# An fp32 encoder layer: operand splits moved between the steps of a projection, one product moved behind a transpose, and the last store halved

## The chip, the cores and the metric

The kernel runs on one core of one Trainium2 chip. The metric is the time of one execution on the device in microseconds (us). The kernel before took 962.0 us, the median of three runs (960.95 to 962.44). The engines are named as the profile names them: PE is TensorE, PEld its weight loads, DVE is VectorE, ACT is ScalarE, POOL is GpSimd, SP is SyncE, which issues nearly all the transfers.

## The reference

One encoder layer is applied to a prompt of 256 tokens and, with the same weights, to a sample of 2048 tokens. The model width D is 1024, every value is fp32. Cut to what matters:

```python
def fourier_mix(u, w_f, b_f):
    ug = u.reshape(b, s, 8, 64)
    spec = jnp.fft.fft2(ug, axes=(1, 3), norm='ortho')
    mixed = spec.real.reshape(b, s, 512)
    return mixed @ w_f + b_f

def encoder_layer(x, w_in, rpb, w_fourier, b_fourier, g_pre, g_na, g_f, w_out, g_post):
    h = rms_norm(x, g_pre)
    q, k, v, z_a, u_f, z_f = jnp.split(h @ w_in, 6, axis=-1)      # 512 columns each
    y_a = neighbourhood_attention(q, k, v, rpb)   # 8 heads of 64; grid 64 wide; window 8 rows x 16 columns
    y_f = fourier_mix(u_f, w_fourier, b_fourier)
    mixed = jnp.concatenate([rms_norm(y_a, g_na) * jax.nn.silu(z_a),
                             rms_norm(y_f, g_f) * jax.nn.silu(z_f)], axis=-1)
    return x + rms_norm(mixed @ w_out, g_post)
```

## The kernel before

**Products of two halves.** An fp32 operand is split into a high part, rounded to the type fp32r, and a low part, the rest. A product of two operands is then three matmuls (`mm3`, L163 to L166): high by high (L164), high by low (L165), low by high (L166). To split an operand, ACT casts it to the high part and DVE subtracts that from the source; the low part can be used when DVE is done. In the names of tiles an h or l at the end stands for the high or low part.

**The order of the work.** PE runs its work in the order in which the program is written. From L604 on this holds for ACT, DVE, POOL and SP as well: each takes its instructions strictly in the written order, and one that waits holds up all behind it on its engine. A helper such as `n_first` writes one instruction for ACT and one for DVE, so where it is called decides what stands behind it on two engines. Tiles come from pools of a fixed number of buffers, and a load into a reused buffer waits for the buffer's last reader.

**Stages by time.** Up to 94 us the first tiles are loaded and part of the values is computed. From 94 to 118.5 us come the prompt's products: a loop over b from 0 to 15, each round 24 matmuls of 256 columns. From 118.5 to 157 us `vu(0, ...)` makes v and u for a group of sample tokens, in 14 steps (j, s) of 12 matmuls of 512 columns. This is a fast scheme that needs seven products where eight would be usual, and j numbers them. Product j has an operand of tokens and an operand of weights:

- The operand of tokens j is written by `n_first(j)`: ACT casts `xh` at L434 and DVE subtracts `xl` at L435, both 128x2048. The source is one of the tiles `nx` and `nt`.
- The operand of weights j is loaded by `op_load(j)` (SP, L469, two halves) and split by `op_split(j)`: ACT L483 and DVE L484, two instructions of 128x1024 each, for j=5 L479 and L480 instead. The tiles are `vr` (raw), `vh` and `vl`.

Product j is first needed at step 2j. PE's results are added up by DVE at L511; finished tiles `vuo` are stored by SP at L354 (`vN`, `uN`). Besides, `rows_load` (SP, L295) brings further tokens `xm` and `rows_square` (ACT, L300) sums their squares. What is called between two steps stands in a table of hooks; within one step the hooks run behind the loads and splits of weights, in the order in which they were entered.

From 157 to 549 us the products for z, k and q and for the rest of the tokens follow. From 549 to 570 us comes the stage called Z here, the first part of the Fourier mix. `z_mm(g)` makes 16 matmuls into two PSUM tiles `ptb` (L1028), which are copied to `zt` (L1031), one by DVE and one by ACT (the first group: both by DVE). `z_turn(g)` transposes these (L1038, into `pab`) and splits the result (ACT L1004, DVE L1005). `z_32` (L1019) makes the one odd column and splits it (ACT L1009, DVE L1010). `pq(m)` multiplies the Fourier weights `wf` by a small matrix of cosines (m=0) or sines (m=1) with eight matmuls (L1081) into `ppq`. For m=1 each of its two halves is copied by ACT to `nq` (L1087), a row set of which POOL sends to `nw` by DMA (L1088); ACT then casts the scaled high part (L1089) and DVE makes the low part (L1090). The column of `nw` is cast at L1107 after `pq(0)`. At 570 us the products with these weights (`py`) start.

From 600 to 860 us the neighbourhood attention runs, from 860 us on the output products with the norm and the residual. `last_tile` ends the program: its second half is computed in two unequal parts to shorten the end, then `residual` (DVE L1758) makes x plus the scaled output for 512 columns and SP stores them (L1763), twice.

Of the kernel before, what the change touches and what calls it, by code (L numbers as in the profile page):

```python
# [168 lines left out]
def build(tc, A, O):  # L169
# [49 lines left out]
    def mmt(n):  # L219
        x = mmc[0] % 5 > 2  # L220
        mmc[0] += 1
        return ps.tile([128, n], F32, tag="t" if x else "a", name="mm", bufs=2 if x else 3)
# [10 lines left out]
    def gt(shape, dtype, name):  # L233
        return gp.tile(shape, dtype, tag="g", name=name)
# [12 lines left out]
    def k8(dtype, name, shape=(128, 4, 512)):  # L247
        return hp.tile(list(shape), dtype, tag="k8", name=name, bufs=NK)
# [142 lines left out]
    def n_load(x):  # L391
        if type(x) is tuple:
            nq[x] = k8(F32, "nx")
            nc.sync.dma_start(nq[x], A["xq"][0, x[0], x[1]])
            return
        nx = [k8(F32, "nx") for kh in range(2)]
        for kh in range(2):
            for b in range(2):
                nq[x, kh, b] = nx[kh][:, 2 * b:2 * b + 2]
                nc.sync.dma_start(nq[x, kh, b], A["xq"][1, kh, b][:, 2 * x:2 * x + 2])  # L400
# [30 lines left out]
    def n_first(j):  # L431
        src = nq[((0, 0), (1, 0), (0, 0), (0, 1), "t3", (1, 0), (1, 1))[j]]
        h, l = bnew[0, j] = [k8(F32R, "x" + x) for x in "hl"]
        nc.scalar.copy(h, src)  # L434
        nc.vector.tensor_tensor(out=l, in0=src, in1=f_(h), op=ALU.subtract)  # L435
# [22 lines left out]
    def r_put(x):  # L458
        nc.sync.dma_start(sD[x], (RU[1], RV[0], RU[0], RU[1], RV[1])[x])
# [3 lines left out]
    def op_load(j):  # L463
        if j < 2:
            l = [load(US, A["wv"][j][:, 2 * x:2 * x + 2], "vr") for x in range(2)]
        else:
            l = [gt(US, F32R, "vl") for x in range(2)]
            for x in range(2):
                nc.sync.dma_start(f_(l[x]), sD[(3, 2, 1, 0, 4)[j - 2]][:, 2 * x:2 * x + 2])  # L469
        op_[j] = [None, l]  # L470
# [228 lines left out]
    def wz_load(n):  # L699
        for x in range(n):  # L700
            wp_.append(load(BS, A["wz"][len(wp_)], "wr"))
# [59 lines left out]
    for b in range(16):  # L761
        kind, blk = divmod(b, 4)
        if 1 <= b < 10:
            wz_load(1)
        if b == 2:
            n_load((1, 1))
        if b in (5, 7):
            r_put(b // 2 + 1)
        if b == 10:
            op_load(0)  # L770
        if b == 12:
            op_load(1)
        if 2 <= b < 14:
            b_raw(b + 2)
        if 2 <= b < 8:
            x, y = divmod(b, 2)
            n_scale(None, *divmod(x, 2)[::-1], range(2 * y, 2 * y + 2))
        elif 8 <= b < 12:
            n_sum(b - 8)
        if b in (5, 12):  # L780
            n_first((5, 12).index(b) + 1)
        if b > 13:
            op_split(b - 14)
        p = mmt(512)[:, :TP]
        wh, wl = wb.pop(b)
        for k in range(KC):
            mm3(nc, p, wh[:, k], wl[:, k], hp_[:, k], lp_[:, k], k == 0, k == KC - 1)
        o = st.tile([128, 256], F32, tag="f", name="f", bufs=3)
        if kind % 2:
            i, d = p, o  # L790
        else:
            i = p.rearrange("p (b r c) -> p b r c", b=2, c=32)
            d = o.rearrange("p (r b c) -> p b r c", b=2, c=32)
        nc.scalar.activation(d, i, AF.Silu if kind < 2 else AF.Copy)
        if kind < 2:
            nc.sync.dma_start(zD[kind, blk * 128:blk * 128 + 128, :TP], o)
        else:
            nc.sync.dma_start((kD if kind == 2 else qD)[blk, :, :TP], o)

    def call(f, *a):  # L800
        return lambda: f(*a)
# [11 lines left out]
    def at(i, f, *a):  # L813
        hooks.setdefault(i, []).append(call(f, *a))

    for x, i in zip(range(3, 7), (0, 3, 5, 7)):
        at(i, n_first, x)
    for x in range(4):
        at(2 * x + 1, rows_load, x + 5)
        at(2 * x + 4, rows_square, x + 5)  # L820
# [19 lines left out]
    for i in range(16):  # L840
# [47 lines left out]
        for j in range(7):  # L888
            for f, d in ((u_load, 0), (u_split, 4), (u_stage1, 6)):
                x = 7 * pr + j - 7 - d  # L890
# [31 lines left out]
            if sg == 0:  # L922
                x, y = divmod(7 * (pr - 1) + j, 14)
# [99 lines left out]
    def z_mm(gq):  # L1023
        for x in range(2):
            for g in range(2 * x, 2 * x + 2):
                for m in range(2):
                    ms = slice(64 * m, 64 * m + 64)
                    nc.tensor.matmul(ptb[x][ms, g % 2 * 256:g % 2 * 256 + 256], d2[gq // 2][:, gq % 2 * 4 + g, ms],  # L1028
                                     zgs[gq][g][:, 256 * m:256 * m + 256], start=True, stop=True)
            zt[gq, x] = sm.tile([128, 512], F32, tag="zt", name="zt", bufs=4)  # L1030
            (nc.scalar.copy if x and gq else nc.vector.tensor_copy)(zt[gq, x], ptb[x])  # L1031

    def z_turn(gq):
        for j in range(2):
            p = ps.tile([128, 4, 128], F32, tag="a", name="pab")
            for g in range(4):
                j0 = g % 2 * 256 + j * 128
                nc.tensor.transpose(p[:, g], zt[gq, g // 2][:, j0:j0 + 128], ident)  # L1038
            split_ps(lambda a: a[:, j::2, :1024].rearrange("p m (k q x) -> p q m k x", k=16, q=4)[:, gq]
                     .rearrange("p m k (g l) -> p m k g l", l=4), p.rearrange("p g (m k l) -> p m k g l", m=2, l=4))  # L1040
# [35 lines left out]
    def pq(m):  # L1076
        h, l = PQ[m] = gt([128, 2, 512], F32R, "pqh"), gt([128, 2, 512], F32R, "pql")
        for c in range(2):
            p = ps.tile([128, 512], F32, tag="b", name="ppq", bufs=2)
            for x in range(2):  # L1080
                nc.tensor.matmul(p[64 * x:64 * x + 64], cs2[:, m, :], wf[c][:, x, :], start=True, stop=True)  # L1081
            if m == 0:
                nc.scalar.copy(h[:, c], p)
                nc.vector.tensor_tensor(out=l[:, c], in0=p, in1=f_(h[:, c]), op=ALU.subtract)
                continue
            nq_ = sm.tile([128, 512], F32, name="nq", bufs=2)
            nc.scalar.copy(nq_, p)  # L1087
            nc.gpsimd.dma_start(nw[16 * c:16 * c + 16:4], nq_[::32])  # L1088
            nc.scalar.activation(h[:, c], p, AF.Copy, scale=dnyq[:, 2:3])  # L1089
            nc.vector.scalar_tensor_tensor(out=l[:, c], in0=p, scalar=dnyq[:, 2:3], in1=f_(h[:, c]),  # L1090
                                           op0=ALU.mult, op1=ALU.subtract)
# [3 lines left out]
    z_mm(1)  # L1095
    z_turn(0)
    z_32(0, 1)
    pq(1)
    z_mm(2)
    z_turn(1)  # L1100
    z_mm(3)
    z_turn(2)
    z_32(2, 3)
# [170 lines left out]
    for t, (g, x) in enumerate(zip(G, (0, 640))):  # L1274
        g["w"] = []
        for c0, w in g["t"]:
            n = 2 * g["nr"] * w
# [348 lines left out]
    for k in range(2, len(G) + 1):  # L1626
        pr, i = divmod(k, 9)
# [20 lines left out]
        x = k // 2 + 1  # L1648
# [65 lines left out]
        if 32 <= k < 36:  # L1714
            x, d = k - 32, atiles[k - 32]
# [35 lines left out]
        V.tensor_scalar(x, y, s, y, ALU.mult, ALU.mult)  # L1751
        V.tensor_scalar(s, x, 1.5, y, ALU.add, ALU.mult)

    def residual(d, n):
        of, xt, s = d["of"], d["xt"], d["r"][:, 0:1]
        ns = slice(n * 512, n * 512 + 512)
        if "og" in d:
            V.scalar_tensor_tensor(out=xt[:, ns], in0=d["og"][:, ns], scalar=s, in1=xt[:, ns], op0=ALU.mult,  # L1758
                                   op1=ALU.add)
        else:  # L1760
            V.scalar_tensor_tensor(out=of[:, ns], in0=ptb[n], scalar=s, in1=of[:, ns], op0=ALU.mult, op1=ALU.mult)
            nc.gpsimd.tensor_tensor(out=xt[:, ns], in0=of[:, ns], in1=xt[:, ns], op=ALU.add)
        nc.sync.dma_start(O["yo"][d["t"] * 128:d["t"] * 128 + 128, ns], xt[:, ns])  # L1763


    def last_tile(d, b):
        og = d["og"] = gt([128, D], F32, "og")
        nc.gpsimd.tensor_tensor(out=og[:, :512], in0=d["of"][:, :512], in1=gpb[:, :512], op=ALU.mult)
        for q, ns in enumerate((slice(512, 896), slice(896, 1024))):
            p = ps.tile([128, 384], F32, tag="a", name="pl", bufs=3)[:, :ns.stop - ns.start]  # L1770
            for j in range(12):
                c, x = divmod(j, 3)
                nc.tensor.matmul(p, (d["l"] if x == 2 else d["h"])[:, c], WO[x == 1][:, c, ns], start=j == 0,
                                 stop=j == 11)
            if q == 0:
                factor(b)
            residual(b, q)
            evac(d, p, ns, 1 + 2 * q)
        sa = d["sa"]
        V.tensor_scalar(sa[:, 0:1], sa[:, 0:1], sa[:, 1:2], None, ALU.add)  # L1780
        part_sum(sa)
        guess(d, 3)
        V.tensor_tensor(out=og[:, 512:], in0=ptb[1], in1=d["of"][:, 512:], op=ALU.mult)
        factor(d, 3)
        for n in range(2):
            residual(d, n)

    for j, d in enumerate(atiles):
        if j + 3 < 18:
# [46 lines left out]
```

## Time and profile before

| What | Value |
|---|---|
| median of 3 runs | 962.0 us (960.95 to 962.44) |
| the profiled execution | 961.61 us |
| its span in the profile | 959.8 us |
| PE busy | 948.7 us, 99% of the span |
| DVE busy | 707.3 us, 74% |
| ACT busy | 496.0 us, 52% |
| POOL busy | 433.9 us, 45% |
| mean granted clock of PE | 0.998 of full speed |

The span runs from the first instruction to the last; 1.8 us of the profiled execution lie around it. A row of a timeline gives the start and the length in us, the engine, the line, the operation and the tiles (written <- read), and in brackets the idle time ahead of it with what ended it. Matmuls overlap: one of 512 columns is shown as 0.39 us long while the next starts 0.23 us after it, so what PE loses is read from the distance of the starts. Rows of one line that follow one another are drawn together, with their count behind the x.

### The profile page before, as it was taken

What the parts mean: (1) busy time and instruction counts of PE and PEld (TensorE: products, weight loads), DVE (VectorE), ACT (ScalarE), POOL (GpSimd) and SP (SyncE); (2) the same over time, 40 slices, a digit from 0 to 9 for tenths busy, and PEclk for the clock granted to TensorE, in tenths of its full rate; (3) what the DMA queues carried; (4) which work ended last, traced back from release to release, by engine and by line L of the source; (5) the groups of instructions that cost most, each with busy time, mean ns of one, the idle gap of its engine ahead of it and who ended that gap; (6) DMA issues with size and microseconds to landing.
All of it is one profiled execution on the core that took longest, in us unless ns stands there. A gap on an engine that the chain in (4) does not pass through costs nothing.

```text
span 959.8 us, 16743 instructions
## 1 busy us (share of the span) xinstructions
PE 948.7 (99%) x5625; PEld 789.3 (82%) x5625; DVE 707.3 (74%) x1296; ACT 496.0 (52%) x1069; POOL 433.9 (45%) x411
## 2 busy tenths in 40 slices
PE   9999999999999999999999999999999999999997
PEld 7889987888888888888888779788788888888885
DVE  6758978687886865698887369776665656659997
ACT  6835676423334532233344267677676766644443
POOL 4100002455661302575566045567678686524544
PEclk9999999999999999999999999999999999999999
DMA  9799696558758984499889996698877998989993
GB/s 357 294 382 335 243 360 219 188 204 292 271 214 315 334 320 148 174 347 350 310 289 347 334 331 243 205 261 269 271 231 251 272 293 265 291 277 348 332 339 135
DMA packets 139933, 269.80 MB, mean 281 GB/s; under 512 B 13162, under 2 KB 80192, under 8 KB 136584
## 3 DMA queue, kind: packets, MB, share of 16 engines
q1 hardware_dynamic: 139496, 268.32, 80.4%
q8 instruction: 45, 0.74, 0.3%
q10 hardware_dynamic: 288, 0.40, 0.1%
q14 instruction: 40, 0.33, 0.1%
q0 software_dynamic: 64, 0.02, 0.0%
HBM read 179.00 MB, written 96.81 MB: 287 GB/s over the span
## 4 chain that ended last, share of the span: by engine, by line
PE 94%; DMA 3%; DVE 1%; ACT 1%; issue 0%; SPq 0%; DVEq 0%
PE po L1481 20%; PE mm L165 17%; PE mm L166 17%; PE mm L164 17%; PE pv L1570 6%; PE ptb L1554 6%; PE s L1214 4%; DMA vl<-sD 1%; DMA xm<-xm 1%; PE py L164 1%; PE py L165 1%; PE py L166 1%; PE ptb L1028 1%; DMA x<-x 0%; DVE vl L484 0%; PE pz L165 0%
## 5 line engine op out<-in xcount | busy, mean ns | idle before, releaser
L164 PE MATMUL mm<-xh,wa 128*128 128x512 f32 x448 | 174.4, 389 | 0.0
L165 PE MATMUL mm<-xl,wa 128*128 128x512 f32 x448 | 174.3, 389 | 0.0
L166 PE MATMUL mm<-xh,wa 128*128 128x512 f32 x448 | 174.3, 389 | 0.0
L538 POOL TENSOR_TENSOR ws<-wr 128x512 f32<-128x512 f32 x16 | 23.2, 1447 | 223.9 <-DMA wr<-wz 211.3
L1248 POOL TENSOR_SCALAR w<-w,m 128x465 f32<-128x465 f32 (+9 forms) x136 | 84.9, 637 | 46.0 <-DVE m L1245 35.5
L165 PEld LDWEIGHTS mm<-xl,wa 128*128 128x128 f32 x448 | 84.1, 188 | 17.6
L164 PEld LDWEIGHTS mm<-xh,wa 128*128 128x128 f32 x448 | 84.1, 188 | 17.5
L166 PEld LDWEIGHTS mm<-xh,wa 128*128 128x128 f32 x448 | 84.1, 188 | 17.4
L1481 PE MATMUL po<-wo,yh 128*128 128x512 f32 x272 | 90.5, 413 | 0.0
L553 DVE TENSOR_TENSOR wa<-wr,wa 128x512 fp32r<-128x512 f32 x60 | 73.3, 1230 | 21.7 <-ACT wa L552 21.4
L1481 PE MATMUL po<-w,yh 128*128 128x512 f32 x280 | 86.8, 391 | 0.0
L1241 ACT ACTIVATE w<-w,m 128x465 f32<-128x465 f32 (+9 forms) x136 | 78.3, 579 | 13.6 <-DVE m L1236 13.3
L1236 DVE CUSTOM_DVE_ANT_1 w<-s,tb 128x465 f32<-128x465 f32 (+8 forms) x124 | 61.2, 532 | 10.1 <-PE s L1214 9.4
L165 PE MATMUL mm<-vl,xh 128*128 128x512 f32 x168 | 65.5, 390 | 1.0 <-DVE vl L480 1.0
L166 PE MATMUL mm<-vh,xl 128*128 128x512 f32 x168 | 65.4, 389 | 0.0
L164 PE MATMUL mm<-vh,xh 128*128 128x512 f32 x168 | 65.4, 389 | 0.0
L591 POOL TENSOR_TENSOR mt<-mt,rmask 128x880 f32<-128x880 f32 (+2 forms) x24 | 50.3, 2110 | 31.8 <-DVE mt L587 19.8
L1481 PEld LDWEIGHTS po<-w,yh 128*128 128x128 f32 x280 | 52.2, 188 | 11.0 <-issue 0.4
L1558 DVE COPY pt<-ptb 120x384 f32<-120x384 f32 (+5 forms) x72 | 40.5, 563 | 27.6 <-PE ptb L1554 27.3
L878 DVE TENSOR_TENSOR f<-u,mm 128x512 f32<-128x512 f32 x64 | 43.4, 678 | 22.1 <-PE mm L166 18.4
L1554 PE MATMUL ptb<-ident,w 128*120 128x128 f32 (+8 forms) x422 | 58.9, 276 | 0.0
L552 ACT CAST wa<-wr 128x512 fp32r<-128x512 f32 x60 | 36.5, 618 | 43.1 <-PE mm L166 19.8
(280 smaller groups left out, 2377.0 us busy)
## 6 DMA issues: line engine op xcount, KB each, us to landing
wr<-wz SPq DMA_DIRECT2D x48, 512.0 KB
vl<-sD SPq DMA_DIRECT2D x20, 512.0 KB
xm<-xm SPq DMA_DIRECT2D x9, 1024.0 KB
oD<-ofs SPq DMA_DIRECT2D x18, 512.0 KB
of<-oD SPq DMA_DIRECT2D x18, 512.0 KB
yr<-yD SPq DMA_DIRECT2D x34, 256.0 KB
zD<-f SPq DMA_DIRECT2D x16, 512.0 KB
xD<-nx SPq DMA_DIRECT2D x14, 512.0 KB
```

Of the source, the lines that this page charges most:

```text
L164: nc.tensor.matmul(out, lh, rh, start=first, stop=False)
L165: nc.tensor.matmul(out, lh, rl, start=False, stop=False)
L166: nc.tensor.matmul(out, ll, rh, start=False, stop=last)
L553: nc.vector.tensor_tensor(out=o[:, 1], in0=src, in1=o[:, 0].bitcast(F32), op=ALU.subtract)
L591: nc.gpsimd.tensor_tensor(out=o, in0=i, in1=rmask[:, m0:m0 + n].unsqueeze(2).to_broadcast([128, n, 80]), op=ALU.add)
L878: nc.vector.tensor_tensor(out=dst(f, b), in0=src(uu[u]), in1=src(p), op=op)
L1236: nc.vector.tensor_tensor_reduce(out=rows(g["w"][b][:, h, :n], w), in0=rows(g["s"][2 * b + h][:, :nr * sw(w)], sw(w))[:, :, :w], in1=tv, s ...
L1241: nc.scalar.activation(w, w, AF.Exp, bias=m[:, h:h + 1], scale=-1.0, accum_out=m[:, 2 + h:3 + h])
L1248: nc.gpsimd.tensor_scalar(w, w, m[:, 4 + h:5 + h], 1.0, ALU.mult, ALU.mult)
L1481: nc.tensor.matmul(p, (d["l"] if x == 2 else d["h"])[:, c], w(n, int(x == 1), c), start=j == 0, stop=j == 11)
L1554: nc.tensor.transpose(ptb[h][:nk, j * 128:j * 128 + 128], g["w"][b][:, h, c0:c0 + nk], ident)
L1570: nc.tensor.matmul(p[hs, b], g["v"][:nk, v, hs], g["pt"][b][:nk, h, j * 128:j * 128 + 128], start=j == 0, stop=j == len(ch) - 1)
```

## The change

Three edits, all of order or of cutting.

**The splits of tokens.** `n_first(3)`, called in step 0 before, is now called in round b=13 of the prompt's loop, ahead of the first two splits of weights (b=14 and b=15). `n_first(4)`, `(5)` and `(6)`, called in steps 3, 5 and 7 before, are now called in steps 0, 3 and 6. In step 6 the hook of `n_first(6)` is entered ahead of `rows_square(6)`.

On DVE at the end of the prompt's loop and in the first steps of `vu(0, ...)` there stand before and now (L435 the split of tokens, L572 the split of the prompt's weights, L484 and L480 splits of the weights of `vu`, L511 the evacuation of its products):

```order
 L435 TENSOR_TENSOR xl<-nx,xh 128x2048
 L572 SCALAR_TENSOR_TENSOR wl<-wr,wh 128x1024
+L435 TENSOR_TENSOR xl<-nx,xh 128x2048
 L484 TENSOR_TENSOR vl<-vr,vh 128x1024 x4
-L435 TENSOR_TENSOR xl<-nx,xh 128x2048
+L435 TENSOR_TENSOR xl<-nt,xh 128x2048
 L484 TENSOR_TENSOR vl<-vl,vh 128x1024 x2
 L511 TENSOR_TENSOR vuo<-uc,mm 128x512
-L435 TENSOR_TENSOR xl<-nt,xh 128x2048
+L435 TENSOR_TENSOR xl<-nx,xh 128x2048
 L511 TENSOR_TENSOR vuo<-uc,mm 128x512
```

One L435 now stands ahead of the four L484 that make the first two operands of weights; behind them each L435 is that of the next operand.

Further on, still on DVE, the steps 5 to 10 of `vu(0, ...)` read:

```order
-L511 TENSOR_TENSOR uc<-uc,mm 128x512
+L511 TENSOR_TENSOR uc<-uc,mm 128x512 x2
+L484 TENSOR_TENSOR vl<-vl,vh 128x1024 x2
 L435 TENSOR_TENSOR xl<-nx,xh 128x2048
-L511 TENSOR_TENSOR uc<-uc,mm 128x512
-L484 TENSOR_TENSOR vl<-vl,vh 128x1024 x2
-L511 TENSOR_TENSOR u_1479<-uc,mm 128x512
-L435 TENSOR_TENSOR xl<-nx,xh 128x2048
+L511 TENSOR_TENSOR u_1483<-uc,mm 128x512
 L511 TENSOR_TENSOR u_1500<-uc,mm 128x512
 L480 SCALAR_TENSOR_TENSOR vl<-vl,vh 128x1024 x2
```

The last L435, that of operand 6, stood between two evacuations right ahead of the two L480 of operand 5; now it stands ahead of both.

On ACT, in the same steps (L434 the casts of tokens, L300 the squares, L483 and L479 the casts of weights):

```order
 L434 CAST xh<-nx 128x2048
 L483 CAST vh<-vl 128x1024 x2
 L300 ACTIVATE xm,ssq<-xm 128x1024 x2
+L483 CAST vh<-vl 128x1024 x2
 L434 CAST xh<-nx 128x2048
+L300 ACTIVATE xm,ssq<-xm 128x1024 x2
 L479 ACTIVATE vh<-vl 128x1024 x2
 L300 ACTIVATE xm,ssq<-xm 128x1024 x2
```

The last L434 stood behind the two L300 of one load of `xm`; now it stands ahead of them.

**The sine weights.** `pq(1)` is called after `z_turn(1)` and not ahead of `z_mm(2)`. On PE in stage Z:

```order
 L1038 MATMUL pab<-ident,zt 128x128 x8
 L1019 MATMUL pab<-d_4688,zg 32x64 x8
-L1081 MATMUL ppq<-wf,cs_102 64x512 x4
 L1028 MATMUL ptb<-zg,d_4690 64x256 x8
 L1038 MATMUL pab<-ident,zt 128x128 x8
+L1081 MATMUL ppq<-wf,cs_102 64x512 x4
 L1028 MATMUL ptb<-zg,d_4690 64x256 x8
 L1038 MATMUL pab<-ident,zt 128x128 x8
```

The matmuls of `pq(1)` move behind those of `z_mm(2)` and `z_turn(1)`. On DVE in the same place (L1090 the low part of the sine weights, L1031 the copy of `zt`, L1005 the split of the transposes):

```order
 L1010 TENSOR_TENSOR a_4845<-pab,a_4845 32x4x16x4 x2
-L1090 SCALAR_TENSOR_TENSOR pql<-ppq,dnyq,pqh 128x512 x2
 L1031 COPY zt<-ptb 128x512
 L1005 TENSOR_TENSOR abl<-pab,abh 128x2x16x16 x2
+L1090 SCALAR_TENSOR_TENSOR pql<-ppq,dnyq,pqh 128x512 x2
 L1031 COPY zt<-ptb 128x512
```

The two L1090 move behind the copy of `zt` and the split of `z_turn(1)`.

**The last store.** In `last_tile` the residual and the store of the second half are done in two pieces of 256 columns. DVE gets one instruction more and SP one store more, and the rows of the two last stores are 1 KB long in DRAM instead of 2 KB.

The diff:

```diff
@@ the prompt's loop
-        if b in (5, 12):
-            n_first((5, 12).index(b) + 1)
+        if b in (5, 12, 13):
+            n_first((5, 12, 13).index(b) + 1)
@@ the hooks of vu(0, ...)
-    for x, i in zip(range(3, 7), (0, 3, 5, 7)):
-        at(i, n_first, x)
+    for x in range(4, 7):
+        at(3 * x - 12, n_first, x)
     for x in range(4):
         at(2 * x + 1, rows_load, x + 5)
         at(2 * x + 4, rows_square, x + 5)
@@ stage Z
     z_mm(1)
     z_turn(0)
     z_32(0, 1)
-    pq(1)
     z_mm(2)
     z_turn(1)
+    pq(1)
     z_mm(3)
     z_turn(2)
     z_32(2, 3)
@@ residual
-    def residual(d, n):
+    def residual(d, n, ns=None):
         of, xt, s = d["of"], d["xt"], d["r"][:, 0:1]
-        ns = slice(n * 512, n * 512 + 512)
+        ns = ns or slice(n * 512, n * 512 + 512)
@@ last_tile
-        for n in range(2):
-            residual(d, n)
+        for ns in (slice(0, 512), slice(512, 768), slice(768, 1024)):
+            residual(d, 0, ns)
```

## The prediction

> **What bounds the kernel now.** I read the page first, its busy times and the chain that ended last.
>
> ```profile
> span 959.8 us, 16743 instructions
> PE 948.7 (99%) x5625; PEld 789.3 (82%) x5625; DVE 707.3 (74%) x1296; ACT 496.0 (52%) x1069; POOL 433.9 (45%) x411
> PE 94%; DMA 3%; DVE 1%; ACT 1%; issue 0%; SPq 0%; DVEq 0%
> ```
>
> PE is busy for 99% of the span and the chain runs over it for 94%. The change takes no matmul away, so it can only win what PE waits for, and the end behind PE. The next view is the list of PE's waits.
>
> ```profile
> PE mm L164 <- ACT xh L289: 1.2, 1, 1.2
> PE idle L231 <- POOL onesq L227: 1.0, 1, 1.0
> PE mm L165 <- DVE vl L480: 1.0, 1, 1.0
> PE ptb L1028 <- DVE zt L1031: 0.8, 1, 0.8
> ```
>
> There are four, each met once. The first two belong to tiles of the program's first part, which the change does not touch. The last two stand in `vu(0, ...)` and in stage Z, the places of the first two edits. Their price and their cause come from the timelines of PE, DVE and ACT around them, and the rest from those of the tail.
>
> **Edit 1, the gain.** In step 10 PE's rows read:
>
> ```profile
> 140.28 0.39 PE L164 MATMUL mm<-vh,xh 128*128 128x512 f32 x1
> 140.51 0.39 PE L165 MATMUL mm<-vl,xh 128*128 128x512 f32 x1
> ...
> 145.72 0.39 PE L164 MATMUL mm<-vh,xh 128*128 128x512 f32 x1
> 147.07 0.50 PE L165 MATMUL mm<-vl,xh 128*128 128x512 f32 x1 [0.97 <-DVE vl L480]
> 147.41 0.40 PE L166 MATMUL mm<-vh,xl 128*128 128x512 f32 x1
> ```
>
> The first two, of step 8, show the undisturbed distance of 0.23 us. From 145.72 to 147.07 are 1.35 us, which loses 1.12, and the next distance of 0.34 loses 0.11: together 1.23 us. What PE waits for is DVE's L480, and why that was late stands in the rows of DVE and ACT:
>
> ```profile
> 143.00 2.29 DVE L435 TENSOR_TENSOR xl<-nx,xh 128x2048 fp32r<-128x2048 f32 x1 [1.71 <-ACT xh L434]
> 145.80 2.35 DVE L480 SCALAR_TENSOR_TENSOR vl<-vl,vh 128x1024 fp32r<-128x1024 f32 x2
> ```
>
> ```profile
> 138.98 1.06 ACT L300 ACTIVATE xm<-xm 128x1024 f32<-128x1024 f32 x1 [1.46 <-DMA xm<-xm]
> 141.07 1.89 ACT L434 CAST xh<-nx 128x2048 fp32r<-128x2048 f32 x1
> 142.87 2.00 ACT L479 ACTIVATE vh<-vl 128x1024 fp32r<-128x1024 f32 x2
> ```
>
> Read backwards: L480 came at 145.80, behind the split of operand 6 (L435), which had let DVE idle for 1.71 us for its cast L434; the cast stood behind the squares L300, and these had waited 1.46 us for a load. Operand 6 is not needed before step 12, so it held up step 10 for nothing. With the change L434 runs ahead of these L300 and L435 two steps earlier. ACT then goes from L300 straight to L479 at about 141.1, whose first half is done at about 142.1. On DVE L480 has only the evacuation of step 8 ahead of it, possible when PE ends that step (140.28 + 12 x 0.227 = 143.0), so L480 starts at about 143.8 and its first half ends at about 145.0. PE asks for it at 145.72 + 0.23 = 145.95. The wait goes, with about a microsecond to spare: −1.23 us.
>
> **Edit 1, the price.** The split of operand 3 moves ahead of the first splits of weights.
>
> ```profile
> 112.28 2.28 DVE L435 TENSOR_TENSOR xl<-nx,xh 128x2048 fp32r<-128x2048 f32 x1
> 114.48 1.22 DVE L572 SCALAR_TENSOR_TENSOR wl<-wr,wh 128x1024 fp32r<-128x1024 f32 x1
> 115.62 4.62 DVE L484 TENSOR_TENSOR vl<-vr,vh 128x1024 fp32r<-128x1024 f32 x4
> ...
> 125.72 2.36 DVE L484 TENSOR_TENSOR vl<-vl,vh 128x1024 fp32r<-128x1024 f32 x2 [2.47 <-ACT vh L483]
> ```
>
> ```profile
> 118.73 0.40 PE L165 MATMUL mm<-vl,xh 128*128 128x512 f32 x1
> ```
>
> DVE runs here without a gap, so an L435 more in the row delays the four L484 by its 2.20 us (112.28 to 114.48). The first, which ended at 115.62 + 1.22 = 116.84, will end at 119.04. PE's second matmul of step 0 reads it at 118.73. It will wait 0.31 us, and from the stall above I add what lies between DVE's end and PE's start there (145.80 + 1.19 = 146.99 to 147.07, so 0.08) and the slow second distance of 0.11: about 0.48 us. The price lies between 0 (if DVE's work ahead packs tighter than I read) and 0.8 (a wait for the second half, too). I take 0.47.
>
> What follows is covered. The fourth row shows DVE idle for 2.47 us at 123.25, so the 2.20 us are made up there. On ACT the moved cast, 1.89 us like that at 141.07, can put off the casts L483 behind it by no more than its length, less than the 2.20 by which DVE comes later anyway. The rest of `vu(0, ...)` slips by some 0.5 us. The tightest margin behind is step 8: PE's L165 at 140.51 needs an L484 whose row is this one:
>
> ```profile
> 138.33 2.36 DVE L484 TENSOR_TENSOR vl<-vl,vh 128x1024 fp32r<-128x1024 f32 x2
> ```
>
> Half of it is done at about 139.55, 0.96 us ahead of its reader. The order puts these L484 ahead of the L435 that stood before them, so DVE does not make them later; the load and the cast ahead of them could. Net of edit 1: −1.23 + 0.47 = −0.76, with ends of −1.23 and, if all the covers fail by a little, 0.
>
> **Edit 2.** Stage Z on PE and DVE:
>
> ```profile
> 554.29 1.09 PE L1038 MATMUL pab<-ident,zt 128*128 128x128 f32 x8
> 555.31 0.71 PE L1019 MATMUL pab<-d,zg 128*32 128x64 f32 x16
> 555.95 1.94 PE L1081 MATMUL ppq<-wf,cs 128*64 128x512 f32 x8
> 557.72 1.90 PE L1028 MATMUL ptb<-zg,d 128*64 128x256 f32 x16
> 559.55 1.10 PE L1038 MATMUL pab<-ident,zt 128*128 128x128 f32 x8
> 561.43 1.95 PE L1028 MATMUL ptb<-zg,d 128*64 128x256 f32 x16 [0.79 <-DVE zt L1031]
> ```
>
> ```profile
> 558.97 0.75 DVE L1090 SCALAR_TENSOR_TENSOR pql<-ppq,dnyq,pqh 128x512 fp32r<-128x512 f32 x1 [0.78 <-ACT pqh L1089]
> 560.03 0.75 DVE L1090 SCALAR_TENSOR_TENSOR pql<-ppq,dnyq,pqh 128x512 fp32r<-128x512 f32 x1 [0.32 <-ACT pqh L1089]
> 560.70 0.68 DVE L1031 COPY zt<-ptb 128x512 f32<-128x512 f32 x1
> ```
>
> A `z_turn` takes 1.02 us from start to start (554.29 to 555.31). `z_turn(1)` began at 559.55, so `z_mm(3)` could have begun at 560.57 and began at 561.43: 0.86 us lost. It overwrites the PSUM tile that DVE copies with L1031, and this copy, whose data was there early in `z_mm(2)`, stood behind the two L1090 of `pq(1)` and their waits for ACT (0.78 and 0.32). After the change `z_mm(2)` starts at 555.95, `z_turn(1)` at 557.78, `pq(1)` at 558.80, `z_mm(3)` at 560.57, and L1031 runs at about 558.2. What is late next is the chain of `pq(1)`, which moves by 2.85 us (555.95 to 558.80) on PE. Its two L1090, some 2 us later than before, end at about 562.8. Behind them on DVE stands the copy of `zt` for `z_turn(3)`, till about 563.4; `z_turn(3)` comes at 560.57 + 1.83 + 1.02 + 0.64 = 564.06 (a `z_mm`, a `z_turn` and a `z_32` by the distances above), so some 0.6 us are to spare. The transfer of `nw` is later as well:
>
> ```profile
> nw<-nq POOLq DMA_DIRECT2D x2, 8.0 KB, 5.0
> 568.70 1.26 ACT L1107 CAST w<-nw 32x512 fp32r<-32x512 f32 x2
> ```
>
> It takes 5.0 us to land, and its last issue, estimated at about 561.7 (behind the second `nq` copy), puts it at 566.7, ahead of L1107 at 568.70 − 0.86 = 567.84. So −0.86, with a gain of nothing at the other end if one of these margins fails.
>
> **Edit 3.** The tail:
>
> ```profile
> 952.74 0.34 DVE L1727 SCALAR_TENSOR_TENSOR of<-pl,inva,of 128x128 f32<-128x128 f32 x1
> ...
> 955.02 1.41 DVE L1758 SCALAR_TENSOR_TENSOR xt<-og,sr,xt 128x512 f32<-128x512 f32 x2
> ```
>
> ```profile
> 955.80 0.33 SPq L1763 DMA_DIRECT2D yo<-xt  x1
> ```
>
> ```profile
> 956.46 0.33 SPq L1763 DMA_DIRECT2D yo<-xt  x1
> ```
>
> ```profile
> GB/s 115 311 442 344 426 360 99 0 0 0 0 0 0 328 360 426 360 393 328 426 360 393 393 344 82 0 0 0 0 0 0 0 0 0 0 0 66 0 0 0
> ```
>
> The last row cuts 955 to 960 us into slices of 0.125 us. The two stores of 256 KB move from slice 13 to slice 24, 956.6 to 958.1, at 328 to 426 GB/s without a gap: the second has its data ready before the first is through. Starting part of the second earlier therefore wins little. One L1758 of 512 columns takes half of 1.41, 0.70 us; 256 columns, between that and the 0.34 of 128 columns, some 0.47. So the third store's data are ready at about 0.70 + 2 x 0.47 = 1.64, against 1.41, 0.2 us later than before, the second's 0.2 earlier. The ends: 0.4 gained, if the shorter last transfer's end counts fully; 0.15 lost, if only the DVE's later end counts. Nearest is the row of the transfers, which shows a stream at its rate: I take −0.10.
>
> The Trainium skill's page "DMA: Bandwidth & Descriptors", in its table of the two cost components, gives a transfer a fixed part of about 2.0 us and a variable one of its bytes over 436e9 a second. Halving the last store would by that save 131072 / 436e3 = 0.30 us, an estimate by that page, and the sum would be 0.20 lower than mine. The same page, section "Why small descriptors are slow (HBM only)", names a fixed overhead for each packet, which speaks against the rows of 1 KB. That the link runs full until 958.1 in the slices above is why I stay below the rule; the rule's 0.30 lies within the 0.4 of the first rival.
>
> **The sum.** −0.76 − 0.86 − 0.10 = −1.72 us. The profiled execution took 961.61 us (its span and 1.8 around it), so the changed kernel would take 959.9 by that; the median of the runs is 0.4 higher, 962.0, and from it 960.3 follows, which I forecast. A measurement of this kernel cannot tell less than about 0.2%, 1.9 us, from no change, so the sum ends just inside that line.
>
> **The rivals.**
>
> 1. More is won. DVE does not hold up step 0, since the rows ahead of L484 close up by more than they show, and the tail pays its 0.4: −1.23 − 0.86 − 0.4 = −2.5, so 959.5. Against it: in the rows above, each of the instructions starts where the one before ends.
> 2. A wait only moves, or an edit doesn't do what it says. If step 10 still waits, now for the load of operand 5 or its cast, the sum is −1.72 + 1.23 = −0.5: 961.5. If `pq(1)` only hands its wait to `z_turn(3)`, it is −0.9: 961.1. For it: each margin there is near a microsecond or below. Against it: the cast that would have to be late (L479) follows L434 without idle time, so its load was there before.
> 3. It is slower. SP issues in order, and a store of finished tiles stands ahead of the loads of the operands 4 to 6 and waits for DVE:
>
> ```profile
> 128.71 0.32 SPq L354 DMA_DIRECT2D vN<-vuo  x1
> ```
>
>    If more splits stood ahead of the evacuation that it stores, the loads would slip by 2.29 us for each and PE would wait in the steps 8, 10 and 12. From a slip of 0.96 on PE loses; at 0.96 + 1.72 the gain is eaten; two splits and the slip of step 0 (2 x 2.29 + 0.47 = 5.05) would cost 4.1 and give 960.3 + 4.1 = 964.4. Against it: in the order as many L435 stand between those points as before, one.
>
> **How the numbers follow.** The sum as worked has 0.67; it is spread by the bounds of the step-0 wait and the tail from 959.6 to 961.0, and a little under half of it lies beyond the line of 0.2%. Rival 1 has 0.16, nearly all beyond it; rival 2 has 0.10, all within; rival 3 has 0.07. Faster by over 0.2%: 0.67 x 0.46 + 0.15 = 0.46; slower: 0.07; within: 0.47. The range goes down to 959.0, under rival 1 by the spread of the medians, and up to 961.6, over rival 2.
>
> **What would show it.** In the changed profile PE's list of waits has no row for L480 and none for L1028 on `zt`; instead a wait of some 0.3 us of L165 for `vl` L484 at 118.7. L480 starts ahead of 144.5, `z_mm(3)` starts 2.8 us behind `z_turn(1)` (1.02 and the 1.77 of `pq(1)`). The span is 958.1. Wrong would make it a wait of PE of over half a microsecond in the steps 2 to 12, a gap of PE ahead of `z_turn(3)`, or a last store that ends more than 0.4 us from where it did against the last matmul.

## The result

The changed kernel takes 960.0 us, the median of 17 runs (959.53 to 961.15), against 961.6 us for the kernel before (17 runs, 960.95 to 964.16). The ratio is 0.9982 with a 95% interval of 0.9975 to 0.9988: 1.6 us faster. That is just inside the 0.2% that the prediction named as the limit of a measurement, but the interval lies clear of 1: with 17 runs each, a gain of this size can be told from none. The forecast was 960.3. The page of the changed kernel begins:

```profile
span 958.3 us, 16747 instructions
PE 949.5 (99%) x5625; PEld 790.1 (82%) x5625; DVE 704.9 (74%) x1297; ACT 496.0 (52%) x1069; POOL 433.7 (45%) x411
```

PE still fills 99%. Its list of waits shows what went and what came:

```profile
PE idle L231 <- POOL onesq L227: 1.0, 1, 1.0
PE ptb L1554 <- DVE pt L1558: 0.5, 1, 0.5
PE mm L164 <- ACT xh L289: 0.3, 1, 0.3
PE mm L165 <- DVE vl L484: 0.2, 1, 0.2
```

L480 and `zt` are gone, as forecast, and the wait for `vl` L484 has come, as forecast. But there is a wait of 0.5 us at L1554 that the prediction did not have. (L1554 are the transposes of the first attention groups.) Cut at points that both kernels pass, the two profiled executions compare as follows, in us:

| Stretch | Before | After | Difference |
|---|---|---|---|
| start to the first matmul of step 0 | 118.49 | 118.31 | −0.18 |
| from there to stage Z | 431.29 | 430.52 | −0.77 |
| stage Z to the first `py` product | 20.65 | 19.79 | −0.86 |
| from there to the first L1758 | 384.58 | 385.19 | +0.61 |
| from there to the end | 4.80 | 4.48 | −0.32 |

The first row is no work of the change: it is the wait of the first tiles, whose first cast (`xh` L289) ends at 6.04 us before and at 5.84 after, and in the kernels below this differs from one execution to the next, too. Of the terms, edit 1 came out as worked (−0.76 forecast, −0.77 found), edit 2 as well in its own stage (−0.86, −0.86), edit 3 at three times its size (−0.10, −0.32), and 0.61 were given back between 568 and 954 us.

**Edit 1.** PE's rows in step 0 and step 10, and DVE's, of the changed kernel:

```profile
118.31 0.39 PE L164 MATMUL mm<-vh,xh 128*128 128x512 f32 x1
118.92 0.50 PE L165 MATMUL mm<-vl,xh 128*128 128x512 f32 x1 [0.22 <-DVE vl L484]
119.25 0.40 PE L166 MATMUL mm<-vh,xl 128*128 128x512 f32 x1
...
146.02 0.39 PE L164 MATMUL mm<-vh,xh 128*128 128x512 f32 x1
146.25 0.39 PE L165 MATMUL mm<-vl,xh 128*128 128x512 f32 x1
146.47 0.39 PE L166 MATMUL mm<-vh,xl 128*128 128x512 f32 x1
```

```profile
115.45 2.28 DVE L435 TENSOR_TENSOR xl<-nx,xh 128x2048 fp32r<-128x2048 f32 x1
117.65 4.62 DVE L484 TENSOR_TENSOR vl<-vr,vh 128x1024 fp32r<-128x1024 f32 x4
...
140.53 2.29 DVE L435 TENSOR_TENSOR xl<-nx,xh 128x2048 fp32r<-128x2048 f32 x1 [2.23 <-ACT xm L300]
...
143.94 2.35 DVE L480 SCALAR_TENSOR_TENSOR vl<-vl,vh 128x1024 fp32r<-128x1024 f32 x2
```

Step 0 loses 0.38 + 0.10 = 0.48 us (0.61 and 0.33 for two distances of 0.23), and step 10 runs at its pitch. L480 starts at 143.94. One thing is not as told: the last L435 is 2.5 us earlier than before but still waits 2.23 us, now for L300. That is no wait for data: the cast that it reads (L434) had run from 136.50 to 138.41. Its `xl` goes into a buffer that the squared tile `xm` leaves free (DVE waits there for the semaphore of that tile's load, too), so the split of operand 6 still follows those squares.

**Edit 2.** Stage Z runs at its pitch, and the copy of `zt` stands ahead of the two L1090:

```profile
556.87 1.09 PE L1038 MATMUL pab<-ident,zt 128*128 128x128 f32 x8
557.89 1.94 PE L1081 MATMUL ppq<-wf,cs 128*64 128x512 f32 x8
559.66 1.90 PE L1028 MATMUL ptb<-zg,d 128*64 128x256 f32 x16
```

```profile
557.26 0.69 DVE L1031 COPY zt<-ptb 128x512 f32<-128x512 f32 x1
...
560.23 0.75 DVE L1090 SCALAR_TENSOR_TENSOR pql<-ppq,dnyq,pqh 128x512 fp32r<-128x512 f32 x1 [0.76 <-ACT pqh L1089]
```

**What was given back.** PE at L1554, 33 us behind the end of stage Z, before:

```profile
603.04 0.60 PE L1554 MATMUL ptb<-ident,kh 128*80 128x128 f32 x4
603.97 0.66 PE L1554 MATMUL ptb<-ident,kh 128*80 128x128 f32 x4
```

and after:

```profile
601.21 0.60 PE L1554 MATMUL ptb<-ident,kh 128*80 128x128 f32 x4
602.14 0.39 PE L1554 MATMUL ptb<-ident,kh 128*80 128x128 f32 x2
603.00 0.39 PE L1554 MATMUL ptb<-ident,kh 128*80 128x128 f32 x2 [0.47 <-DVE pt L1558]
```

Here PE is 1.83 us earlier than before, but DVE, which has to copy `pt` (L1558), only 1.1, as its L1403 shows:

```profile
598.14 0.68 DVE L1403 TENSOR_TENSOR y0h<-y,y0h 128x512 fp32r<-128x512 f32 x1
```

```profile
597.04 0.69 DVE L1403 TENSOR_TENSOR y0h<-y,y0h 128x512 fp32r<-128x512 f32 x1
```

Followed back, DVE and ACT lose the difference at one instruction: ACT's L1292, which splits the first output weights `wo` and waits for their load. Its rows, before and after:

```profile
578.20 1.34 ACT L1292 ACTIVATE wo<-wr,gmix 128x512 fp32r<-128x512 f32 x2 [1.07 <-DMA wr<-wo]
```

```profile
577.13 1.34 ACT L1292 ACTIVATE wo<-wr,gmix 128x512 fp32r<-128x512 f32 x2 [1.82 <-DMA wr<-wo]
```

The wait grew from 1.07 to 1.82 us. The load stands at the end of a row of loads for the attention whose first (K, L1121) waits on SP until the last stores of z have landed, as SP's list of waits for 553 to 582 us shows for the changed kernel:

```profile
SPq L1121 <- DMA zD<-f: 4.6, 1, 4.6
```

These stores are issued when the products before stage Z end. Edit 1 moves that point and edit 2 does not: counted from the start of stage Z, the weights land after 28.40 us before and after 28.28 with all edits. My theory for the experiments (A) was therefore: edit 2 brings PE forward against loads that stay, and part of its gain is lost at L1554. The rival (B): DVE's work from 572 to 602 us is full by itself, or edit 1 is what causes the wait.

### The profile page after: what moved, and what is told of

It reads as the page before. It is cut to its first block, busy times and chain, and to the rows that moved or that the text cites. A ratio compares the mean times of both kernels' runs of the same rounds, so it can differ in the third digit from the quotient of the medians.

```text
span 958.3 us, 16747 instructions
## 1 busy us (share of the span) xinstructions
PE 949.5 (99%) x5625; PEld 790.1 (82%) x5625; DVE 704.9 (74%) x1297; ACT 496.0 (52%) x1069; POOL 433.7 (45%) x411
## 4 chain that ended last, share of the span: by engine, by line
PE 92%; DMA 3%; DVE 2%; ACT 1%; issue 1%; SPq 0%; POOL 0%; DVEq 0%
PE po L1481 20%; PE mm L165 18%; PE mm L164 18%; PE mm L166 18%; PE pv L1570 6%; PE ptb L1554 6%; PE s L1214 4%; DMA wr<-wo 1%; DMA za<-zD 1%; DMA zD<-f 1%; DVE Y L1323 0%; DMA x<-x 0%; PE pz L164 0%; PE pz L165 0%; PE pz L166 0%
## 5 line engine op out<-in xcount | busy, mean ns | idle before, releaser
L553 DVE TENSOR_TENSOR wa<-wr,wa 128x512 fp32r<-128x512 f32 x60 | 70.3, 1180 | 21.7 <-ACT wa L552 21.4
L1558 DVE COPY pt<-ptb 120x384 f32<-120x384 f32 (+5 forms) x72 | 40.5, 563 | 27.8 <-PE ptb L1554 27.7
L1554 PE MATMUL ptb<-ident,w 128*120 128x128 f32 (+8 forms) x422 | 58.8, 276 | 0.0
```

The source lines that it names most:

```text
L553: nc.vector.tensor_tensor(out=o[:, 1], in0=src, in1=o[:, 0].bitcast(F32), op=ALU.subtract)
L1554: nc.tensor.transpose(ptb[h][:nk, j * 128:j * 128 + 128], g["w"][b][:, h, c0:c0 + nk], ident)
```

## The experiments

All times in us; each kernel was measured in five rounds beside the kernel before. The stretches are those of the table above, from one profiled execution of each kernel.

| Kernel | Median (before beside it) | Ratio, 95% interval | Step 0 to Z | Z to `py` | `py` to L1758 | L1758 to end |
|---|---|---|---|---|---|---|
| before | 961.6 | | 431.29 | 20.65 | 384.58 | 4.80 |
| all edits | 960.0 (961.6) | 0.9982, 0.9975 to 0.9988 | 430.52 | 19.79 | 385.19 | 4.48 |
| edit 1 alone | 960.92 (961.66) | 0.9991, 0.9982 to 1.0 | 430.53 | 20.65 | 384.57 | 4.80 |
| edit 2 alone | 960.91 (961.66) | 0.9993, 0.9984 to 1.0001 | 430.84 | 19.79 | 384.84 | 4.79 |
| edit 3 alone | 961.24 (961.66) | 0.9993, 0.9984 to 1.0002 | 431.12 | 20.65 | 384.59 | 4.48 |
| all, table later | 959.72 (961.66) | 0.9978, 0.9969 to 0.9986 | 430.54 | 19.79 | 384.59 | 4.48 |
| only operand 6 moved | 960.35 (961.5) | 0.9986, 0.9978 to 0.9995 | 431.47 | 19.79 | 384.76 | 4.47 |
| the same, table later | 959.75 (961.5) | 0.9983, 0.9974 to 0.9992 | 430.72 | 19.79 | 384.58 | 4.47 |
| first half of store cut | 961.1 (961.5) | 0.9994, 0.9985 to 1.0003 | 431.40 | 20.65 | 384.60 | 4.58 |
| both halves cut | 961.98 (961.5) | 1.0007, 0.9998 to 1.0016 | 431.47 | 20.65 | 386.58 | 5.21 |
| operand 3 in step 0 | 960.2 (961.68) | 0.9981, 0.9972 to 0.999 | 430.47 | 19.79 | 385.53 | 4.48 |
| the same, table later | 959.73 (961.68) | 0.9986, 0.9977 to 0.9994 | 430.03 | 19.79 | 384.86 | 4.47 |

The intervals of the three single edits reach 1 or come to it, so what one edit is worth is read from the stretches and not from the medians. Two of the stretches repeat well: Z to `py` takes 20.65 us in the five kernels without edit 2 and 19.79 in the seven with it; the end takes 4.79 or 4.80 in the three with the old stores and 4.47 or 4.48 in the seven with edit 3.

### Edit 1 alone

```diff
-        if b in (5, 12):
-            n_first((5, 12).index(b) + 1)
+        if b in (5, 12, 13):
+            n_first((5, 12, 13).index(b) + 1)
...
-    for x, i in zip(range(3, 7), (0, 3, 5, 7)):
-        at(i, n_first, x)
+    for x in range(4, 7):
+        at(3 * x - 12, n_first, x)
```

> Edit 1 alone (the splits of tokens). Theory A: it wins 1.24 us in step 10 and pays 0.48 in step 0, net -0.76 us; the stores and loads behind it move along with PE, so no wait of L1554 on DVE's L1558 appears near 602 us, and the span ends 0.7 to 0.8 us below the kernel before (beyond what the first tiles' waits differ from run to run). Rival B: whatever brings PE to 602 us earlier meets a DVE that does not come earlier; then some 0.6 us of it are lost there and the net is -0.1 to -0.2.

From step 0 to stage Z it takes 0.76 us less, and nothing is lost behind (384.57). The wait at L1554 does not come from edit 1: theory A.

### Edit 2 alone

```diff
     z_32(0, 1)
-    pq(1)
     z_mm(2)
     z_turn(1)
+    pq(1)
```

> Edit 2 alone (the products of the sine weights). Theory A: 0.87 us are won by 565 us, but the loads of stage Z start when the stores of the last products land, which this edit does not move; the weights wr<-wo land as before, ACT's L1292 behind them starts within 0.2 us of where it did, DVE comes to its L1558 no earlier, and PE waits some 0.6 to 0.8 us at L1554 near 603 us: net -0.1 to -0.3. Rival B: the wait at L1554 in the changed kernel comes from edit 1; then edit 2 keeps its 0.87.

Stage Z is 0.86 us shorter and the wait at L1554 is there without edit 1, but it costs 0.26, less than expected:

```profile
602.64 0.39 PE L1554 MATMUL ptb<-ident,kh 128*80 128x128 f32 x2
603.22 0.39 PE L1554 MATMUL ptb<-ident,kh 128*80 128x128 f32 x2 [0.19 <-DVE pt L1558]
```

```profile
577.60 1.34 ACT L1292 ACTIVATE wo<-wr,gmix 128x512 fp32r<-128x512 f32 x2 [1.76 <-DMA wr<-wo]
```

L1292 waits 1.76 us for its load, as with all edits. Rival B in its second form falls. How much of the lateness reaches PE differs between executions of the same order: in the four kernels with edit 2 and the table in its old place it is 0.61 (all edits), 0.26 (here), 0.18 (only operand 6 moved) and 0.67 us (operand 3 in step 0), though the weights land 27.9 to 28.3 us behind the start of stage Z in all of them. Why it differs stays open. In this execution step 10 also waited 0.45 us less than in the profile of before, with the same splits: its cause, the load of `xm`, had landed earlier (see below).

### The second bias table loaded later

The table of 1200 KB (L1139) is used by later attention groups; here its load is issued behind the first two loads of output weights.

```diff
-    load_t(0, 1)
     wo1 = [[gt([128, 2, 512], F32R, "wo1") for c in range(4)] for n in range(2)]
...
     for c in range(2):
         wo1_load(c)
+    load_t(0, 1)
```

> All edits, and the load of the second bias table (1200 KB, L1139) is issued behind the first two loads of output weights and not ahead of them. Theory A: the weights land 1.5 to 3 us earlier, L1292 starts by more than 1 us earlier, the wait of L1554 on L1558 near 602 us goes, and the span is 0.5 to 0.6 us below that of the changed kernel. Rival B: DVE's row of work from 572 to 602 us is full by itself, L1292 or not; then the wait at L1554 stays and nothing changes (within 0.1 us).

L1292, here L1291, starts 1.7 us earlier and without waiting, and PE's four transposes run through:

```profile
575.42 1.32 ACT L1291 ACTIVATE wo<-wr,gmix 128x512 fp32r<-128x512 f32 x2
```

```profile
602.35 0.66 PE L1554 MATMUL ptb<-ident,kh 128*80 128x128 f32 x4
```

The stretch from `py` to L1758 is back at 384.59, 0.60 less than with all edits. The weights land 24.8 us behind the start of stage Z here. So the load's landing is the cause, shown by taking it away. The medians differ by less, 0.3 us (959.72 against 960.0), and the intervals of the two ratios overlap.

### Edit 3 alone

```diff
-        for n in range(2):
-            residual(d, n)
+        for ns in (slice(0, 512), slice(512, 768), slice(768, 1024)):
+            residual(d, 0, ns)
```

> Edit 3 alone (the last store in two pieces). From the start of the first L1758 to the end of the span were 4.78 us before and 4.49 with all edits. The page's rule (bytes over 436e9 a second for the last transfer) gives -0.30; the prediction's term gave -0.10, by the reading that the stream of both stores was limited by its rate. The rest of the span unchanged.

The end is 0.32 us shorter, as with all edits. That agrees in size with the 0.30 by the Trainium skill's page "DMA: Bandwidth & Descriptors" (table of the two cost components, which the page draws for transfers issued by POOL; these are SP's). But the trace's landings do not bear out its reason here: counted from the start of the first L1758, the last bytes land after 3.47 us before, after 3.56 here and 3.57 with all edits, later by 0.1, about what DVE needs for one instruction more (1.54 against 1.41). The last store is issued 0.24 us later than before and takes 0.14 less to land. What is shorter lies behind the landing. There SP runs through its final checks of semaphores (L1831), the counters that tell of landed transfers and finished instructions, and its first DRAIN follows them. Before, and with all edits:

```profile
L1831 SPq DRAIN  x3: 7/7/28, 959.0 to 959.3; - x3
```

```profile
L1831 SPq DRAIN  x3: 7/7/7, 957.5 to 957.8; - x3
```

The landings were at 958.49 and 957.37: half a microsecond ahead of the first DRAIN before, a tenth now. The trace's records of SP show why. Between two checks that have nothing to wait for there are some 0.06 us from start to start, but at one place in the row 0.36 to 0.38. Before, this place came behind the check that waits for the last store; with one store more it comes earlier in the row and passes while the stores are under way. Two kernels test this, one with the last store whole and one with four stores.

### First half cut, and both halves cut

```diff
-        for n in range(2):
-            residual(d, n)
+        for ns in (slice(0, 256), slice(256, 512), slice(512, 1024)):
+            residual(d, 0, ns)
```

> The kernel before with the first, not the last, 512 columns of the last residual and store cut in two. The last store keeps its 256 KB. By the rule of bytes for the last transfer nothing is won at the end (0.0 beyond an earlier start of the stream, at most 0.2). The other reading: in the cut kernel the last bytes land no earlier (3.56 us behind the start of L1758, before 3.47); what is shorter is SP's row of final checks behind them, 0.15 us against 0.57, since the last store's semaphore is then the last that SP checks. With three stores it is that here, too: by this the span after the start of L1758 is shorter by 0.3 to 0.5 us, as with the last store cut.

```diff
-        for n in range(2):
-            residual(d, n)
+        for ns in (slice(0, 256), slice(256, 512), slice(512, 768), slice(768, 1024)):
+            residual(d, 0, ns)
```

> The kernel before with both halves of the last residual and store cut in two: four stores of 128 KB. By the rule of bytes the end is as with the last one cut, -0.3 us, or 0.1 to 0.2 better by the earlier start. By the reading of SP's final checks the last of four stores has a semaphore that SP checks early, with five checks behind it: 0.3 to 0.6 us lie between the landing and the end of the checks, and the gain against the kernel before is 0.2 or less.

Their first DRAINs:

```profile
L1831 SPq DRAIN  x3: 7/7/7, 958.7 to 959.0; - x3
```

```profile
L1831 SPq DRAIN  x3: 7/7/7, 961.4 to 961.7; - x3
```

From the start of the first L1758, in us:

| Stores | Last bytes land | from there to SP's second DRAIN | to the end |
|---|---|---|---|
| 256, 256 KB (before) | 3.47 | 0.57 | 4.80 |
| 256, 128, 128 KB (edit 3) | 3.56 | 0.15 | 4.48 |
| 128, 128, 256 KB | 3.67 | 0.15 | 4.58 |
| 128, 128, 128, 128 KB | 3.68 | 0.76 | 5.21 |

With the last store whole, 0.22 us are won, though its bytes land 0.20 later: less than the 0.3 to 0.5 expected, because I had not counted the later landing. With four stores the last one is half as large as before and the end comes 0.41 later; its semaphore is checked early, and five checks and the slow place stand behind it. The median of eleven runs, 961.98 against 961.5, points the same way, but its interval includes 1. (The 2.0 us more in the stretch ahead of it belong to the one profiled execution, 963.98, in which the attention lost them from 805 to 814 us.) No cut made the last bytes land earlier than before. What edit 3 gains from is thus the row of final checks, 0.57 to 0.15; the size of the last store counts for 0.10 only, by which 128 KB at the end land earlier than 256 KB among three stores.

The traces also show what the slow place is bound to: the count of SP's records. In five kernels (before, edits 1 and 2 alone, and the two of this section) the pause stands ahead of the same record of SP, the 1232nd of the trace; in the other seven SP waits at that record for a store. In the kernel with 128, 128, 256 KB this is the fifth check: it comes at 2.52 us, 0.36 behind the fourth, though the store that it asks for had landed at 2.22. Counted back from there in steps of 128 records, SP pauses at every one of these places for at least 0.34 us, in all twelve kernels; at each of the other 127 places of that period the shortest pause is 0.05. A store more puts two more records (a wait and an issue) ahead of the checks, so the pause meets a check that stands two earlier. Why SP pauses there stays open.

### Only operand 6 moved

All edits, but operand 3, 4 and 5 stay in steps 0, 3 and 5, and operand 6 goes to step 6.

```diff
-    for x, i in zip(range(3, 7), (0, 3, 5, 7)):
+    for x, i in zip(range(3, 7), (0, 3, 5, 6)):
         at(i, n_first, x)
```

> All edits, but of the splits of tokens only operand 6 is moved (step 7 to step 6, ahead of the squares); operand 3 stays in step 0, 4 and 5 stay in steps 3 and 5. Theory A: the wait of step 10 comes from operand 6 alone and the price of step 0 from operand 3 alone; then neither L480 nor the first L484 makes PE wait, and from step 0 to stage Z the kernel takes 0.48 us less than with all edits. Rival B: without the earlier operands 4 and 5, DVE comes to L480 late again and step 10 keeps a wait of 0.3 to 1.2 us.

The price of step 0 is gone and the wait of step 10 is back in full, 1.38 us, so nothing is won by it: 431.47. Rival B was right, and the reason is the buffer:

```profile
142.57 2.29 DVE L435 TENSOR_TENSOR xl<-nx,xh 128x2048 fp32r<-128x2048 f32 x1 [1.20 <-ACT xm L300]
144.78 1.28 DVE L511 TENSOR_TENSOR u<-uc,mm 128x512 f32<-128x512 f32 x2
145.98 2.35 DVE L480 SCALAR_TENSOR_TENSOR vl<-vl,vh 128x1024 fp32r<-128x1024 f32 x2
```

```profile
138.54 1.92 ACT L434 CAST xh<-nx 128x2048 fp32r<-128x2048 f32 x1 [0.46 <-DVE xl L435]
140.36 1.06 ACT L300 ACTIVATE xm<-xm 128x1024 f32<-128x1024 f32 x1
```

The last L435 needs the buffer that the two L300 at 140.36 free, and these come 2 us later than with all edits (138.32 there), since ACT first casts operand 5 in step 5 and operand 6 waits for it. The prediction's account of edit 1, that operand 6 alone held up step 10, was too short: it has to move together with operands 4 and 5 (whether both are needed was not tried).

The same kernel with the table loaded later:

> The kernel of the run above with the second bias table loaded behind the output weights. By theory A of both runs: no wait of PE but the two at the program's start, 1.0 to 1.1 us less than with all edits as they were (0.48 of step 0, 0.6 of L1554). Rival: PE, earlier by 0.48, meets another late transfer in stage Z or later and keeps half of it or less.

It lost 0.62 us in step 10 and nothing at L1554 (384.58), and takes 959.75 us. Step 10 is as in the run above but for the load of `xm`, which landed 1 us earlier. The wait differs from execution to execution: in the five profiles that have the splits of before, step 10 loses 0.75 to 1.40 us.

### Operand 3 back in step 0

All edits, with operand 3 split in step 0 ahead of operand 4.

```diff
-    for x, i in zip(range(3, 7), (0, 3, 5, 7)):
-        at(i, n_first, x)
+    for x in range(3, 7):
+        at(max(0, 3 * x - 12), n_first, x)
```

> All edits, but the split of operand 3 stays in step 0 (ahead of that of operand 4); 4, 5 and 6 are in steps 0, 3 and 6 as changed. Theory A: the price of step 0 (0.48 us) comes from operand 3 standing ahead of the first L484 alone, and the wait of step 10 is gone since operands 5 and 6 come earlier; DVE's idle time of 1.56 us ahead of the L484 at 126.03 takes up the later L435. Then PE waits neither in step 0 nor in step 10, and from step 0 to stage Z the kernel takes 0.48 us less than with all edits. Rival B: the moved L435, or the copies L514 behind two casts on ACT, now hold up step 4 or the loads behind SP's first store, and 0.3 us or more of it are lost again by step 12.

The wait of step 0 is gone and a part of step 10's is back: its two distances are 0.49 and 0.34, so 0.37 us of 0.48 are lost again. That is the loss of rival B, but its cause, the splits, is not shown: a load of `vl` had landed late in this execution, so that L480 started 0.9 us later than with all edits, and the next kernel has the same splits and no such wait. Two waits stand in the attention:

```profile
PE ptb L1554 <- DVE pt L1558: 0.6, 1, 0.6
...
PE ptb L1554 <- ACT nsb L1530: 0.3, 1, 0.3
```

The second, at 623 us, is new; its cause stays open. The same kernel with the table loaded later:

> The kernel of the run above with the second bias table loaded behind the output weights. Theory A: no wait of PE but the two at the program's start; 0.48 + 0.6 = 1.1 us less than with all edits, a median near 958.9. Rival B: PE, earlier by 0.48 us against loads that it does not move, waits again somewhere from stage Z on, and the gain is 0.6 or less.

```profile
PE idle L231 <- POOL onesq L227: 1.0, 1, 1.0
PE mm L164 <- ACT xh L289: 0.5, 1, 0.5
PE ptb L1554 <- ACT nsb L1530: 0.3, 1, 0.3
```

Here step 0 and step 10 run at their pitch, 430.03 us to stage Z, the least of all, and the wait on L1558 is gone; the one on L1530 keeps 0.28. From step 0 to the end it takes 0.83 us less than with all edits, in the profile. Its median is 959.73, that of the kernel with the table alone 959.72: the two cannot be told apart, nor, since the intervals of the ratios overlap, either of them from the change with its 960.0.

## Why the prediction was right, and where it was not

- **What bounds.** Right: PE, with two waits that the change could take away, and both went.
- **Edit 1, the gain.** Right in size (step 10 at its pitch; L480 at 143.94 against 143.8 worked out). Short in its reason: the split of operand 6 also waits for a buffer that the squares free, so it does not pass them, and moving it alone wins nothing. L480 followed that late split and two evacuations without idle time, which the working did not have; that it came to nearly the same start is luck. So is part of the size: with the old splits step 10 loses 0.75 to 1.40 us, and the 1.23 is one execution of that.
- **Edit 1, the price.** Right: 0.48 us against 0.47 (the three terms as written, 0.31, 0.08 and 0.11, add up to 0.50; the 0.08 is 0.05 in the trace, where the first L480 ends at 147.02), and the 2.20 us on DVE were made up in its idle time (1.56 us of it are left at the same place).
- **Edit 2.** −0.86 in its own stage, as worked out. The step that failed is "what is late next": I followed the chain of `pq(1)` to `z_turn(3)` and to `nw`, which held, and did not ask which loads move along with PE. The output weights did not, and 0.61 us went at L1554. In other executions 0.18 to 0.67 went there. That is rival 2's mechanism at another place; rival 2 had it at `z_turn(3)`.
- **Edit 3.** The term was mis-sized: −0.10 forecast, −0.32 found. The 0.10 was to come from the bytes, and these land 0.09 us later, not earlier. Nor did the stream's rate hold up the second store: the two stores of before take 2.04 and 2.03 us from issue to landing. What the term lacked is what SP does between the last landing and the end, 0.57 us before and 0.15 after.
- **The sum.** −1.72 forecast, −1.6 found between the medians, −1.54 between the profiled executions. Errors cancelled there in part: +0.61 at L1554 against −0.22 more at the tail and −0.18 at the start, which is no work of the change. That the total came so near is luck to that extent. The 960.3 was counted from the 962.0 of three runs; from the 961.6 of 17 runs the same sum gives 959.9.
- **Rivals.** The first had both its halves in view: step 0 did lose time, so that half was wrong, and the tail paid 0.32 of its 0.4. The third, slower by late loads in the steps 8 to 12, did not show here: the loads' margins held. They are thin, as the 0.37 us show that a late load cost in the kernel with operand 3 in step 0.

## What to carry to other kernels

When a wait of the bounding engine is taken away, list the transfers whose issue does not depend on that engine's new, earlier time; the first of them with no slack is where the gain, or a part of it, goes. Of a wait on a split or a copy, ask what it reads and also whose buffer it writes into: an instruction moved forward in its row can still wait for the reader that frees its buffer. At the end of a program, measure from the last landing to the end before paying for smaller stores.

## What the runs showed of the hardware

SP pauses for at least 0.34 us at every 128th of its records in the trace (0.34 to 0.35 where it waits for nothing else), and in these kernels one such place falls into the row of final checks, whose steps are otherwise some 0.06 us. With each store more it stands two checks earlier; whether it is hidden depends on which check waits for the last store. The kernels above agree on it; its cause is open.

The profiled execution of the last kernel began slowly. Eight of PE's first matmuls stand 0.43 us apart, where the others show 0.23:

```profile
8.93 0.63 PE L164 MATMUL mm<-wc,xh 128*128 128x512 f32 x1
9.35 0.63 PE L165 MATMUL mm<-wc,xh 128*128 128x512 f32 x1
...
10.53 0.40 PE L165 MATMUL mm<-wc,xh 128*128 128x512 f32 x1
10.76 0.39 PE L166 MATMUL mm<-wc,xl 128*128 128x512 f32 x1
```

From 7.2 to 10.5 us it runs at about half its rate. The first matmul of step 0 stands at 120.14 us, 1.6 to 2.0 us later than in the other kernels, which is why the span, 959.3 us, says nothing against this one. The trace's record of the granted clock bears it out: full speed begins at 10.39 us here and at 3.9 to 6.8 us in the eleven others. The Trainium skill's page "TensorE: Matmul & The Clock Gate", Part 1, describes a half rate that lasts for about 3.4 us of time after a cold start and varies from run to run. The traces agree that it varies, but not on the length: from PE's first matmul, at 0.99 us, to full speed pass 9.4 us here and 3.0 to 5.8 in the others. The stretches at full speed are 952.32, 948.91 or 945.49 us long, so they differ by steps of 3.41. Four of the eleven runs of this kernel (960.87 to 961.49) lie 0.9 us or more above the other seven (959.48 to 959.93), which would fit, but only one of them was profiled.
